# Longer planned distances in a generated schedule, and two stages moved: a hybrid attention and gating block on one core

## Chip, cores and metric

One core of a Trainium2 chip runs the whole program. The metric is the device time of one execution in microseconds (us); lower is better. Engines are named as in the profile: PE is TensorE, DVE VectorE, ACT ScalarE, POOL GpSimd, SP the engine whose queue issues nearly all transfers.

## What is computed

x is 1024 x 1024, float32, one layer, 8 heads of 64 and 8 gating groups of 64. Cut to what matters:

```python
h = rmsnorm(x, norm_g)
q, k, v, z_a, u_b, v_b, z_b, g_a, g_b = split(h @ w_in)      # 1024 -> 5632
# attention: w[t, s] = sigmoid(z[t, s]) * prod over s < r < t of sigmoid(-z[t, r]), s < t
y_a = stick_breaking_attention(q, k, v) * silu(z_a)          # 1024 x 512
y_b = spatial_gating(gelu(u_b), gelu(v_b), ...) * silu(z_b)  # 1024 x 512
merged = sigmoid(g_a) * (y_a @ w_up_a) + sigmoid(g_b) * (y_b @ w_up_b)
out = rmsnorm(x + merged @ w_out, final_norm_g)
```

## The kernel before

**Matrix products.** Every large product is made of three float32r products of high and low parts (hi x hi, lo x hi, hi x lo), 128 x 128 weights against 512 columns. The high part is a copy on ScalarE, the low part a subtraction on VectorE or GpSimd (`hi_lo`).

**Stages.** First x is normalised, transposed and split (`make_h`), and v is projected (`v_unit`, PSUM tiles X, Y, Z, o). Then come 20 projection groups (`project`), each two tiles of 128 output columns made by a seven-product scheme of 12 matmuls each on tiles T; the raw weights are four loads (tile a), their parts tiles b. What leaves a group goes through `use`: kq groups (keys and queries of two heads) are split and stored, u and zb groups make the gated halves of the spatial branch, vb groups normalise and mix (with `mix_weights` and `make_shift`), za groups make the attention branch's SiLU, g groups make sigmoid gates. Results go to DRAM tiles (d) and are read back where needed: zb reads u, vb reads the product uz, a head reads its kq tiles.

**Heads.** Eight heads h0 to h7 run in turn (`head`, `attn_step`, `attn_row`). A head loads the tiles kh, q, kl and v (tag k, `load_head`). For each row block of 128, z = q x kh + q x kl (PSUM z, two buffers), ScalarE makes two sigmoids (tiles ak and r), VectorE a running product along the row (lines 192 and 199), VectorE or GpSimd the weights; TensorE transposes them by blocks of 128 columns (PSUM tr), ScalarE and VectorE split them (tiles e), and TensorE sums them with v in PSUM o. A head's result goes into tile os; for an odd head it is multiplied by the gate and, but for the last pair, stored.

**End.** The up projections of the spatial branch (`up_b`), those of the attention branch for the first and the second half of the sequence (`up_a`), then the output projection and the last norm.

**Who sets the order.** Nothing is issued as it is written. `Plan.add` records each operation as a task with an engine, a cost and its dependencies. `Plan.issue` (line 235) then plays a table of events: each engine takes, of the tasks that are ready and whose buffers are to be had, the one of lowest priority number, and the order in which tasks were taken is the order in which they are issued, engine by engine, and for transfers in SP's queue. On the chip, semaphores make every dependency hold; the table's times count only through the order.

- Costs are formulas per kind of operation; a transfer costs its bytes at 360 GB/s and 0.02 us (lines 219 to 232).
- A task's users become ready at its end, later by `LAT` (line 24) if they are on another engine; behind a transfer they become ready `tail` after its end (lines 225 and 232).
- A buffer comes free `tail` (0 but for transfers) and `LAT` after its last user's end (line 319). The tags have few buffers: k 6, f1 4, f2 6, a 7, b 8, r 5, ak 4, e 4, z 2, tr 2, and one each of X, Y, Z, o. Buffers of a tag are handed out in the order in which the program first names them.
- A task's priority number is its place in the program. For engines other than TensorE an offset is added: -9000 for a projection's own work, and for the work on its results -6000 if the group is marked `+` (`ahead`), else 0. For TensorE the place in the program counts alone: of two groups that are both ready, the one named earlier goes first, and a later group fills in where the earlier one waits.
- The stages between the v projection and the end are named in this list (lines 831 and 832):

```python
    ORDER = ("+kq0 u0 zb0 vb0 +za0 +u1 zb1 +vb1 h0 h1 kq1 h2 g2 +g0 +kq2 +g1 "
             "+kq3 +za1 h3 h4 h5 g6 g3 h6 g4 g5 h7 +g7")
```

h0 and h1 read kq0, h2 and h3 kq1, h4 and h5 kq2, h6 and h7 kq3; h5 and h7 read the results of za1.

Of the kernel before, what the change touches and what calls it, by code (L numbers as in the profile page):

```python
# [20 lines left out]
EPS = 1e-6  # L21
GELU_C = 0.044715
GELU_S = 1.5957691216057308
LAT = 0.25
SCAN = 2.0


# [53 lines left out]
def raw_words(v):  # L81

    return v.ap().bitcast(F32) if v.buf.dt == F32R else v.ap()
# [7 lines left out]
class Plan:  # L91
# [127 lines left out]
    def load(self, out, dram, queue=None):  # L219
        q = queue or self.nc.sync  # L220
        rows = out.box[0][1] - out.box[0][0]
        view = isinstance(dram, View)
        self.add("DMA", out.n * rows * 4 / 360e3 + 0.02,
                 lambda: q.dma_start(out=raw_words(out), in_=dram.ap() if view else dram), [out], [dram] if view else [],  # L224
                 tail=2.0)

    def store(self, dram, in_, queue=None):
        q = queue or self.nc.sync
        view = isinstance(dram, View)
        self.add("DMA", in_.n * P * 4 / 360e3 + 0.02,  # L230
                 lambda: q.dma_start(out=dram.ap() if view else dram, in_=raw_words(in_)), [dram] if view else [], [in_],
                 tail=2.0)


    def issue(self):
# [26 lines left out]
        while done < len(self.tasks):  # L262
# [38 lines left out]
            while events and events[0][0] <= now + 1e-9:  # L301
# [5 lines left out]
                elif kind == 0:  # L307
                    for u in t.users:
                        lag = t.tail if t.eng == "DMA" else 0.0 if u.eng == t.eng else LAT
                        u.ready = max(u.ready, now + lag)  # L310
# [4 lines left out]
                    for b in t.bufs:  # L315
                        b.left -= 1
                        if b.left == 0 and b.tag in free:
                            seq += 1
                            heapq.heappush(events, (now + t.tail + LAT, seq, 2, b.tag))
        self.length = max(t.end for t in self.tasks)  # L320
# [13 lines left out]
def hybrid_block(  # L334
# [489 lines left out]
    def head(p, h):  # L824
        parts = load_head(p, h)
        for ch in range(2):
            if h == 0:
                sums_of[p, ch] = buf("os")
            attn_step(*parts, p, h, ch, sums_of[p, ch])

    ORDER = ("+kq0 u0 zb0 vb0 +za0 +u1 zb1 +vb1 h0 h1 kq1 h2 g2 +g0 +kq2 +g1 "
             "+kq3 +za1 h3 h4 h5 g6 g3 h6 g4 g5 h7 +g7")
    groups_of = {"kq": make_kq, "u": make_u, "zb": make_zb, "vb": make_vb, "za": make_za, "g": make_gates}
    for word in ORDER.split():
        name = word.strip("+0123456789")
# [200 lines left out]
```

## Time and profile before

| what | us |
|---|---|
| median of 3 runs | 774.28 (771.2 to 777.28) |
| the profiled execution | 775.14 |
| its span, first to last instruction | 773.4 |
| TensorE busy | 739.1 |
| VectorE busy | 559.9 |
| ScalarE busy | 433.8 |
| GpSimd busy | 300.7 |

The profile is of one execution; the 1.7 us between its time and its span lie outside the program's instructions. A busy TensorE is a modelled figure: a 128 x 512 matmul is shown with some 390 ns, and back to back one starts every 0.227 us (12 in 2.72 us). Holes are therefore read from the idle time that a timeline shows in brackets, with what ended it, and from the number of matmuls in a window. A granted clock of 1.00 is the engine's upper level (2.4 GHz), 0.50 its lower one (1.2 GHz).

### The profile page before, as it was taken

The numbers are of one execution on the slowest core, as the hardware profiler recorded it, in microseconds if no ns is written. First come the engines' busy times: TensorE is split into PE (matmuls) and PEld (weight loads), VectorE is DVE, ScalarE is ACT, GpSimd is POOL, SyncE is SP. The second block draws the span as 40 slices with busy tenths as digits, with TensorE's granted clock in tenths as the row PEclk, the third lists the DMA queues.
The fourth block names the chain that finished last, engine by engine and source line by source line (L and its number), as shares of the span: only waits on it lengthen the run. The fifth ranks groups of instructions, "written<-read, shape, count | busy, mean of one in ns | idle before, by whom it ended". The sixth has DMA issues, their size and how long they took to land.

```text
span 773.4 us, 10783 instructions
## 1 busy us (share of the span) xinstructions
PE 739.1 (96%) x3524; PEld 609.9 (79%) x3524; DVE 559.9 (72%) x788; ACT 433.8 (56%) x920; POOL 300.7 (39%) x298
## 2 busy tenths in 40 slices
PE   4998999999999999998999999999899999999996
PEld 3776888778887888787888788788688788888885
DVE  5679454797658887976869997879779898961132
ACT  6655474655656466575666576758557544431122
POOL 1400636586677761642556353260321030003110
PEclk9999999999999999999999999999899999999999
DMA  8503593423354463546247354534986636871022
GB/s 325 192 28 122 176 247 123 149 96 123 106 181 131 160 199 102 161 147 164 93 153 205 109 134 126 149 125 144 259 264 222 212 132 211 261 252 74 28 82 109
DMA packets 69177, 121.31 MB, mean 157 GB/s; under 512 B 7296, under 2 KB 17024, under 8 KB 69120
## 3 DMA queue, kind: packets, MB, share of 16 engines
q1 hardware_dynamic: 67968, 118.52, 48.6%
q10 hardware_dynamic: 1152, 2.10, 0.7%
q8 instruction: 28, 0.46, 0.2%
q14 instruction: 29, 0.24, 0.1%
HBM read 81.27 MB, written 39.32 MB: 156 GB/s over the span
## 4 chain that ended last, share of the span: by engine, by line
PE 80%; DMA 7%; issue 4%; DVE 4%; POOL 3%; ACT 1%; SPq 1%; POOLq 0%; DVEq 0%; ACTq 0%
PE Y L131 20%; PE X L131 20%; PE Z L131 17%; PE z L131 9%; PE o L131 9%; PE tr L135 5%; DMA k<-d 4%; DMA k<-in_x_dram 1%; DVE T L168 1%; POOL a L168 1%; SPq L224 1%; POOL f L168 1%; DMA a<-d 1%; DMA a<-in_w_pairs_dram 1%; DVE b L168 1%
## 5 line engine op out<-in xcount | busy, mean ns | idle before, releaser
L131 PE MATMUL Y<-T,b 128*128 128x512 f32 x672 | 180.6, 399 | 2.8 <-ACT b L159 1.6
L131 PE MATMUL X<-T,b 128*128 128x512 f32 x660 | 177.3, 400 | 0.0
L159 ACT CAST b<-a 128x512 fp32r<-128x512 f32 (+1 forms) x152 | 93.3, 615 | 111.0 <-PE X L131 34.9
L131 PE MATMUL Z<-T,b 128*128 128x512 f32 x540 | 147.6, 398 | 0.0
L131 PEld LDWEIGHTS Y<-T,b 128*128 128x128 f32 x672 | 123.1, 190 | 26.2 <-ACT b L159 2.1
L131 PEld LDWEIGHTS X<-T,b 128*128 128x128 f32 x660 | 121.6, 190 | 22.8
L168 DVE TENSOR_TENSOR b<-a,b 128x512 fp32r<-128x512 f32 (+1 forms) x112 | 94.8, 847 | 50.3 <-ACT b L159 46.4
L131 PEld LDWEIGHTS Z<-T,b 128*128 128x128 f32 x540 | 98.2, 188 | 17.9
L168 POOL TENSOR_TENSOR b<-a,b 128x512 fp32r<-128x512 f32 x40 | 58.7, 1469 | 95.6 <-ACT b L159 89.7
L168 POOL TENSOR_TENSOR f<-f,f 128x512 f32<-128x512 f32 (+1 forms) x38 | 58.3, 1538 | 49.4 <-ACT f L148 23.7
L168 POOL TENSOR_TENSOR a<-a,a 128x512 f32<-128x512 f32 x40 | 59.1, 1478 | 30.3 <-DVE b L168 13.5
L168 POOL TENSOR_TENSOR r<-r,ak 128x512 f32<-128x512 f32 x32 | 44.5, 1396 | 64.7 <-DVE ak L192 48.8
L131 PE MATMUL z<-k,k 128*128 128x512 f32 (+2 forms) x216 | 59.9, 358 | 9.4 <-DMA k<-d 8.6
L159 ACT CAST e<-tr 128x512 fp32r<-128x512 f32 (+1 forms) x96 | 45.8, 480 | 36.3 <-PE tr L135 34.1
L168 DVE TENSOR_TENSOR e<-tr,e 128x512 fp32r<-128x512 f32 (+1 forms) x96 | 52.5, 548 | 16.0 <-ACT e L159 15.6
L199 DVE TENSOR_TENSOR_SCAN ak<-ak,c 128x128 f32<-128x128 f32 (+1 forms) x64 | 63.6, 1001 | 0.2 <-ACT ak L148 0.2
L135 PE MATMUL tr<-c,r 128*128 128x128 f32 x320 | 60.9, 275 | 1.5 <-POOL r L168 1.5
L131 PE MATMUL o<-e,k 128*128 128x512 f32 (+1 forms) x192 | 58.4, 348 | 0.0
L148 ACT ACTIVATE ak<-z 128x128 f32<-128x128 f32 (+2 forms) x96 | 47.2, 493 | 16.8 <-PE z L131 11.6
L131 PEld LDWEIGHTS z<-k,k 128*128 128x128 f32 x216 | 40.1, 192 | 18.8 <-issue 5.5
L148 ACT ACTIVATE r<-z 128x128 f32<-128x128 f32 (+2 forms) x96 | 46.8, 493 | 12.2 <-PE tr L135 11.7
L135 PEld LDWEIGHTS tr<-c,r 128*128 128x128 f32 x320 | 41.7, 141 | 15.0 <-POOL r L168 3.0
(217 smaller groups left out, 1158.1 us busy)
## 6 DMA issues: line engine op xcount, KB each, us to landing
d<-f SPq DMA_DIRECT2D x112, 256.0 KB, 2.7
a<-in_w_pairs_dram SPq DMA_DIRECT2D x80, 256.0 KB, 2.7
f<-d SPq DMA_DIRECT2D x72, 256.0 KB, 3.3
k<-d SPq DMA_DIRECT2D x48, 256.0 KB, 4.3
k<-in_x_dram SPq DMA_DIRECT2D x8, 512.0 KB, 6.8
d<-b SPq DMA_DIRECT2D x16, 256.0 KB, 2.3
k<-d SPq DMA_DIRECT2D x8, 512.0 KB, 6.3
a<-in_w_up_dram SPq DMA_DIRECT2D x16, 256.0 KB, 4.6
```

The lines of the kernel that those rows point to most:

```text
L131: lambda: self.nc.tensor.matmul(out.ap(), lhsT=lhsT.ap(), rhs=rhs.ap(), start=start, stop=stop, **kw),
L135: self.add("PE", 0.109, lambda: self.nc.tensor.transpose(out=out.ap(), in_=in_.ap(), identity=ident.ap()), [out], [in_, ident])
L148: return self.nc.scalar.activation(out=out.ap(), in_=in_.ap(), func=func, scale=sc, **kw)
L159: lambda: self.nc.scalar.copy(out=out.ap(), in_=in_.ap()), [out], [in_])
L168: self.add(eng, cost, lambda: e.tensor_tensor(out=out.ap(), in0=in0.ap(), in1=in1.ap(), op=op), [out], [in0, in1])
L199: lambda: self.nc.vector.tensor_tensor_scan(out.ap(), in_.ap(), floor.ap(), init, op0=ALU.mult, op1=ALU.max), [out], [in_, floor])
L224: lambda: q.dma_start(out=raw_words(out), in_=dram.ap() if view else dram), [out], [dram] if view else [],
```

## The change

`LAT` becomes 0.5, the tail of loads and stores 5.0, and the list names u0 before +kq0, and h3 before +kq3 and +za1. No operation and no buffer is added or taken away.

```diff
-LAT = 0.25
+LAT = 0.5
...
     def load(self, out, dram, queue=None):
...
-                 tail=2.0)
+                 tail=5.0)
 
     def store(self, dram, in_, queue=None):
...
-                 tail=2.0)
+                 tail=5.0)
...
-    ORDER = ("+kq0 u0 zb0 vb0 +za0 +u1 zb1 +vb1 h0 h1 kq1 h2 g2 +g0 +kq2 +g1 "
-             "+kq3 +za1 h3 h4 h5 g6 g3 h6 g4 g5 h7 +g7")
+    ORDER = ("u0 +kq0 zb0 vb0 +za0 +u1 zb1 +vb1 h0 h1 kq1 h2 g2 +g0 +kq2 +g1 "
+             "h3 +kq3 +za1 h4 h5 g6 g3 h6 g4 g5 h7 +g7")
```

## Rows read from the trace of the kernel before

**Rows 1.** The page, parts 1 and 2: busy engines, granted clock in 40 slices.

```profile
PE 739.1 (96%) x3524; PEld 609.9 (79%) x3524; DVE 559.9 (72%) x788; ACT 433.8 (56%) x920; POOL 300.7 (39%) x298
...
PEclk9999999999999999999999999999899999999999
```

**Rows 2.** The page, part 4: chain that ended last, by line.

```profile
PE Y L131 20%; PE X L131 20%; PE Z L131 17%; PE z L131 9%; PE o L131 9%; PE tr L135 5%; DMA k<-d 4%; DMA k<-in_x_dram 1%; DVE T L168 1%; POOL a L168 1%; SPq L224 1%; POOL f L168 1%; DMA a<-d 1%; DMA a<-in_w_pairs_dram 1%; DVE b L168 1%
```

**Rows 3.** Windows of 20 us: length, busy us per engine, clock, DMA share, GB/s.

```profile
60.00:80.00 20.00, 17.17 (x75) 13.61 (x74) 18.98 (x23) 11.36 (x18) 2.20 (x2) 1.00 0.35 123
...
340.00:360.00 20.00, 17.52 (x87) 14.23 (x87) 15.74 (x21) 13.65 (x34) 7.78 (x7) 1.00 0.50 140
...
540.00:560.00 20.00, 16.27 (x67) 13.16 (x66) 14.72 (x19) 11.69 (x27) 6.60 (x5) 0.87 0.93 264
...
620.00:640.00 20.00, 20.00 (x106) 16.68 (x105) 18.71 (x27) 9.36 (x23) 6.39 (x5) 1.00 0.42 146
```

**Rows 4.** Tile z on TensorE: waits in all; then TensorE's timeline, two stretches.

```profile
  DMA k<-d: 8.6, 6
...
359.33 0.30 PE L131 MATMUL z<-k,k 128*128 128x128 f32 x1 [2.48 <-DMA k<-d]
...
555.72 0.45 PE L131 MATMUL z<-k,k 128*128 128x128 f32 x1 [3.73 <-DMA k<-d]
```

**Rows 5.** TensorE's waits: line, releaser, us in all, times, longest.

```profile
PE tr L135 <- POOL r L168: 1.5, 2, 1.0
...
PE z L131 <- ACT r L148: 0.8, 1, 0.8
```

**Rows 6.** Timelines of TensorE at 305 us, of SP's queue at 306 and 352 us.

```profile
307.72 0.63 PE L131 MATMUL z<-k,k 128*128 128x512 f32 x2
...
313.49 0.30 PE L131 MATMUL z<-k,k 128*128 128x128 f32 x1 [0.66 <-DMA k<-d]
...
308.67 1.10 SPq L224 DMA_DIRECT2D k<-d  x2
...
353.26 0.38 SPq L231 DMA_DIRECT2D d<-f  x1
```

**Rows 7.** The page, part 6: DMA issues, median us from issue to landing.

```profile
d<-f SPq DMA_DIRECT2D x112, 256.0 KB, 2.7
...
k<-d SPq DMA_DIRECT2D x48, 256.0 KB, 4.3
```

**Rows 8.** Windows at the two long holes, columns as in rows 3.

```profile
360.40:363.80 3.40, 3.40 (x11) 2.68 (x11) 2.67 (x5) 1.90 (x4) 0.00 (x0) 0.50 1.01 245
...
555.00:561.80 6.80, 6.08 (x19) 5.24 (x20) 1.66 (x3) 1.58 (x5) 1.50 (x2) 0.50 0.95 269
```

**Rows 9.** Timeline of all engines at 47 us.

```profile
47.78 0.59 ACT L159 CAST T<-tr 128x512 fp32r<-128x512 f32 x1 [0.64 <-PE tr L135]
...
48.40 1.89 DVE L168 TENSOR_TENSOR T<-tr,T 128x512 f32<-128x512 f32 x3 [0.34 <-ACT T L159]
```

**Rows 10.** The page, part 5: VectorE's subtract for the weights' low parts.

```profile
L168 DVE TENSOR_TENSOR b<-a,b 128x512 fp32r<-128x512 f32 (+1 forms) x112 | 94.8, 847 | 50.3 <-ACT b L159 46.4
```

**Rows 11.** Tile o on TensorE: matmuls of the heads, and TensorE's idle time.

```profile
L131 PE MATMUL o<-e,k x192: 221/389/628, 299.7 to 649.6; 128*128 128x512 f32 x96, 128*128 128x384 f32 x32, 128*128 128x256 f32 x32, 128*128 128x128 f32 x32
...
  ACT e L159: 1.6, 2
```

**Rows 12.** Timelines of SP, ScalarE and TensorE at 138 to 141 us.

```profile
137.83 0.45 SPq L224 DMA_DIRECT2D f<-in_sgu_ln_b_dram  x1
...
140.92 0.30 ACT L159 CAST e<-f 128x128 fp32r<-128x128 f32 x1 [2.62 <-DMA f<-in_sgu_ln_b_dram]
...
141.28 0.39 PE L131 MATMUL o<-b,e 128*128 128x256 f32 x1 [1.16 <-ACT e L159]
```

**Rows 13.** TensorE's timeline where the last head ends.

```profile
649.56 0.39 PE L131 MATMUL o<-e,k 128*128 128x512 f32 x1
...
657.72 0.39 PE L131 MATMUL Y<-T,T 128*128 128x512 f32 x1
```

## The prediction

> **What bounds the kernel now.** I read the page's busy shares and slices first. TensorE is busy 739.1 of 773.4 us; VectorE, the next, 559.9 [rows 1]. The chain that ended last runs mostly over TensorE's lines, and 4% of it is the load of a head's tiles, k<-d, the largest entry that is not TensorE's [rows 2]. Then the 20 us windows, for where TensorE is short of work: 60 to 80 us has 17.17 us busy, 340 to 360 has 17.52 and 540 to 560 has 16.27, while 620 to 640 has 20.00, as all of them have from there to 760 [rows 3]. So what a new order can win lies in single holes before that, and in the granted clock: the slices show 9 everywhere but in one of them [rows 1].
>
> The holes in the heads have one cause. The view of tile z, which every head's first matmuls write, says that TensorE sat idle 8.6 us in 6 places until a k<-d transfer landed; the two longest are 2.48 us before 359.33 and 3.73 us before 555.72 [rows 4]. In the heads' stretch the view of TensorE's waits names little else: 1.5 us on POOL r and 0.8 on ACT r [rows 5].
>
> Why the table misses these: a head takes four tiles k and there are six, so kl and v of the next head can be asked for only when the last z of this one is done. The table then counts 0.25 (LAT) + 2 x 0.73 (two loads of 256 KB at its 360 GB/s) + 2.0 (tail) = 3.7 us to the first matmul on kl, and puts that much projection between. The trace: last z pair starts at 307.72, the loads are issued from 308.67, the matmul on kl starts at 313.49, some 5.2 us after the pair's last matmul (307.72 + 0.23 + 0.3 = 308.25) [rows 6]. A k<-d of 256 KB needs 4.3 us from issue to landing by the median, where the table has 2.73; the stores d<-f of the same size need 2.7 [rows 7].
>
> **The change part by part.** No instruction is added or removed; the three edits only move instructions within each engine's program and within SP's queue.
>
> *Tail 2.0 to 5.0 on loads.* The table's distance to kl grows to 0.5 + 1.46 + 5.0 = 6.96 us, by 3.25. Every one of the six holes shorter than 3.25 us should be filled with projection matmuls, each worth 0.227 us; of the 3.73 us hole 0.5 us is left. 8.6 - 0.5 = **8.1 us saved**. Cover: in each of the seven changes of head some 14 matmuls of projection more must be there to put in. Up to 650 us there are (below).
>
> *The clock.* Directly behind the two long holes the granted clock is at the lower level: 0.50 in 360.40:363.80, where only 11 matmuls start, and 0.50 in 555.00:561.80 with 19 [rows 8]. At half rate, 3.4 us and 6.8 us cost 1.7 + 3.4 = **5.1 us**, which go with the holes. They may stay in part if one hole stays; so between 0 and 5.1, and I take all, since the four shorter holes (8.6 - 2.48 - 3.73 = 2.4 us together) have no such stretch behind them.
>
> *Tail on stores, LAT in the freeing of buffers.* A store's f1, f2 or b buffer counts as taken for 3.25 us longer, so the table hands it out later than the chip does. On the chip the order alone counts, and an order made for later buffers makes nobody wait that did not before; TensorE is given other ready work in that time. I cost it at nothing; if the cover is gone it shows as in the first rival.
>
> *LAT 0.25 to 0.5.* Between engines the chip needs little: VectorE starts at 48.40, 0.03 us after ScalarE ended (47.78 + 0.59) [rows 9]. So 0.25 was long enough where the durations are right; 0.5 gives slack for those that the table has too short: VectorE's subtract b<-a,b takes 847 ns where its formula gives 0.67 us [rows 10]. What it costs in the heads: a block of 128 columns passes TensorE, ScalarE, VectorE and TensorE, three crossings, 0.75 us more in the table; the tiles e (4, two to a block) let two blocks go on together, so 0.375 us a block. The 192 o matmuls [rows 11] are 96 blocks: 36 us of stretch over all heads in the table, if this chain and not VectorE sets a head's pace there. Below: it takes the 1.5 + 0.8 us of short waits away [rows 5]. Above: the order is new everywhere and gets as many short waits again as now. I take the upper end, **2.5 us lost**, for I have no row that says that the new misses will be fewer.
>
> *u0 before +kq0.* In front of zb0 stands then a whole group, 7 products of 2.72 us, instead of nothing, and zb0 reads u back from DRAM. Its reloads take f1 buffers, and vb0's first load into such a buffer, f<-in_sgu_ln_b, is issued only at 137.83; ScalarE waits 2.62 us for it, and TensorE 1.16 us behind ScalarE [rows 12]. All of TensorE's waits for ScalarE at tile o, this one and those of the later vb matmuls, are 1.6 us [rows 11]. kq0 comes 19 us later, its first reader (h0's loads) far behind. Between 0 and 1.6 us saved: I take **0.8**, half, since the buffers are as few as before. In the queues u0's 4 weight loads and 4 stores go ahead of kq0's 4 loads and 8 stores on SP, and the 7 POOL operations of the one ahead of the 7 of the other; nobody else stands between. What 60 to 80 us lacks of 20, 2.8 us [rows 3], stays: whichever group is first finds TensorE waiting until its first weights are split.
>
> *h3 before +kq3 +za1.* TensorE's order is by place in the list, so until now kq3 and za1 went ahead of h3. Now h3 goes ahead of them and 14 products are left over as filler for the heads behind it. Its 7 loads pass in SP's queue the 8 weight loads and 12 stores of the two groups, and need only kq1, stored long before; its 4 POOL products pass work of lower number, which keeps its offset and goes first where it is ready. It moves work, 0 us by itself; it pays some of the time that heads lose through the longer distances.
>
> Sum: -8.1 - 5.1 - 0.8 + 2.5 = -11.5 us. The profiled execution took 775.14 us (span 773.4 and 1.7 around it), so 763.6; it lies 0.9 above the median of 774.28, on which I get 762.8. I say **763 us**.
>
> The Trainium skill has a rule that speaks against the first step: "DMA: Bandwidth & Descriptors", section "Anatomy of one DMA — SWDGE (gpsimd) path", gives one transfer a fixed cost of about 2.0 us and its bytes over 436 GB/s besides, an estimate of 2.6 us for 256 KB. By it the old tail is right, the longer one is needless and nothing is gained. The page's fit is for the GpSimd path and these loads go through SP's queue; the 4.3 us of rows 7 contradict it for k<-d and the 2.7 of the stores agree with it.
>
> **The rivals.** *Heads outlast their filler (slower).* The longer distances keep the heads on for longer while TensorE is fed with projections and up products. What is left when the last head ends is little: its last o is at 649.56, and up to 657.72, where z and the second half's products set in, there are 7.9 us of first-half products [rows 13]. The table adds 7 x 3.25 = 22.75 us at the changes of head and up to 36 us within them, 58.8 in all. If half of it, 29.4 us, reached the chip, TensorE would starve 29.4 - 7.9 = 21.5 us near 650 us, and 775.1 - 11.5 + 21.5 = 785 us. It decides from a stretch of 7.9 + 11.5 = 19.4 us on. For it: VectorE is busy 14.7 to 18.7 of 20 us there [rows 3], so a head can't catch up fast. Against: of the 22.75 us the chip needs the larger part today already (5.2 of 6.96 at each change), and h3 goes earlier.
>
> *Waits that move (no change).* kl lands later still when the order puts other transfers beside it: the DMA share is 1.01 and 0.95 in the stretches where the long holes end [rows 8]. If half of the 8.6 us and the clock's loss stay and the 2.5 us of new waits come, then 775.1 - 4.3 - 0.8 + 2.5 = 772.5 us.
>
> *The old distance was right (no change).* A transfer takes 2.7 us when nothing is beside it, as the stores' row has it [rows 7]; then the holes come of SP's queue, where a store at 353.26 stands ahead of the loads of the hole at 359 [rows 6], and stay: 775 us. The Trainium skill's rule named above would have it so.
>
> **How the numbers follow.** Forecast 0.53; waits that move 0.26; old distance right 0.06; heads outlast the filler 0.15. A measurement of this kernel can tell about 1% from no change, 7.7 us: under 766.5 is faster, over 782.0 slower. The forecast is faster, the two in the middle the same, the last slower: 0.53, 0.32, 0.15. The likeliest one's own range: all gains and no new waits, -8.6 - 5.1 - 1.6 - 2.3 = -17.6, 757; without half of the clock's share and of the holes, 769. For the range of the time I go to 754, for holes before 80 us that may also shut a little, and on the other side to 780, which leaves out most of the last rival.
>
> **What would show it.** Right: the view of tile z names k<-d with under 2 us; no stretch of clock 0.50 after 100 us; windows 340 to 360 and 540 to 560 hold 20.00; the wait of 1.16 us at 141 us is gone; the last head ends later than 649.6 by less than 8 us. The first rival: TensorE idle between 640 and 670 us, waiting for os or T tiles. The second: k<-d's median landing over 5 us and z still waiting. Wrong altogether if z waits less and the time is the same or longer: then the new misses weigh as much as the old.

## The result, and the profile after

| | us |
|---|---|
| before, median | 773.21 |
| changed, median | 761.86 (761.43 to 762.38) |
| ratio | 0.9847, 95% interval 0.9804 to 0.989 |
| span of the profiled execution, before and after | 773.4 and 760.5 |

The changed kernel is 11.4 us, 1.5%, faster; 763 us had been said, within 754 to 780. The median before is of four executions: a fourth of 772.15 us has come to the three behind the 774.28 given above. Both traces are of executions above their medians (775.14 and 762.38 us), so between the traces a little more is won than between the medians. The changed kernel's busy times and its clock, from the page:

```profile
PE 734.5 (97%) x3524; PEld 607.9 (80%) x3524; DVE 563.3 (74%) x788; ACT 432.2 (57%) x920; POOL 304.4 (40%) x298
...
PEclk9999999999999999999999999999999999999999
```

TensorE has the same 3524 matmuls as before and 12.9 us less span [rows 1]; the one slice of clock 8 is gone. Tile z on TensorE, its whole list of waits, beside [rows 4]:

```profile
  DMA k<-d: 0.2, 1
```

The 8.6 us in 6 places are 0.2 in one. The windows that answer to [rows 3]:

```profile
60.00:80.00 20.00, 17.17 (x68) 13.36 (x67) 18.00 (x23) 11.36 (x18) 2.59 (x2) 0.91 0.33 115
...
340.00:360.00 20.00, 20.00 (x102) 16.62 (x100) 15.81 (x26) 14.27 (x35) 2.66 (x6) 1.00 0.41 119
...
540.00:560.00 20.00, 19.91 (x105) 16.50 (x104) 16.87 (x24) 10.89 (x26) 7.45 (x9) 1.00 0.88 280
...
620.00:640.00 20.00, 18.70 (x95) 15.25 (x94) 19.87 (x30) 7.65 (x15) 6.67 (x4) 1.00 0.47 147
```

340 to 360 is full and holds 102 matmuls instead of 87; 540 to 560 has 105 instead of 67 and the clock at 1.00. The holes before 80 us are as before, but the clock behind the one at 70 us is lower (0.91 in this window; the last section comes back to it). What TensorE still waits for, the six longest (line, releaser, us in all, times, longest), beside [rows 5]:

```profile
PE tr L135 <- DVE k L174: 10.3, 2, 7.3
PE Y L131 <- ACT b L159: 2.0, 1, 2.0
PE o L131 <- DVE e L168: 1.5, 2, 1.1
PE X L131 <- ACT r L159: 1.4, 1, 1.4
PE Z L131 <- DVE T L168: 1.3, 1, 1.3
PE tr L135 <- POOL r L168: 1.0, 2, 0.6
```

The first, second and fourth belong to the first 80 us. In the heads' stretch 1.5 + 1.3 + 1.0 = 3.8 us are left. Before it was 1.3 us: 0.8 on ACT r and only 0.5 of the 1.5 us on POOL r [rows 5]. The other 1.0 us of POOL r lies ahead of the heads, which begin at 283.1 us; from the timeline of the kernel before:

```profile
167.86 0.66 PE L135 MATMUL tr<-c,r 128*128 128x128 f32 x4 [1.00 <-POOL r L168]
```

ACT e's 1.6 us [rows 11] lie there too, at 141 and 251 us, and 0.3 us on DVE c at 264: 2.9 us in all, and all of it is gone. So from 100 us on TensorE's waits for anything but k<-d were 4.2 us (2.9 ahead of the heads, 1.3 in them) and are 3.8, all in the heads. Where the last head ends, beside [rows 13]:

```profile
625.77 0.73 PE L131 MATMUL Z<-T,T 128*128 128x512 f32 x2 [1.30 <-DVE T L168]
...
643.29 0.39 PE L131 MATMUL o<-e,k 128*128 128x512 f32 x1
...
645.33 0.62 PE L131 MATMUL z<-T,T 128*128 128x512 f32 x2
```

Between the last o and the first z of the second half's products there are now 2.0 us, where there were 8.6 (from 649.56 [rows 13] to 658.17 in the same timeline); and at 625.77 TensorE stood 1.30 us for a T tile. The cover has shrunk by 6.6 us.

### The profile page after: what moved, and what is told of

It reads as the page before. It is cut to its first block, busy times and chain, and to the rows that moved or that the text cites. A ratio compares the mean times of both kernels' runs of the same rounds, so it can differ in the third digit from the quotient of the medians.

```text
span 760.5 us, 10807 instructions
## 1 busy us (share of the span) xinstructions
PE 734.5 (97%) x3524; PEld 607.9 (80%) x3524; DVE 563.3 (74%) x788; ACT 432.2 (57%) x920; POOL 304.4 (40%) x298
## 4 chain that ended last, share of the span: by engine, by line
PE 85%; DVE 4%; issue 4%; DMA 2%; POOL 2%; ACT 1%; SPq 0%; POOLq 0%; DVEq 0%
PE Y L131 22%; PE X L131 22%; PE Z L131 19%; PE z L131 9%; PE o L131 8%; PE tr L135 5%; DVE T L168 1%; DMA k<-d 1%; DVE ak L192 1%; DMA k<-in_x_dram 1%; POOL a L168 1%; POOL r L168 1%; DMA f<-d 1%; DVE b L168 0%; POOL b L168 0%
## 5 line engine op out<-in xcount | busy, mean ns | idle before, releaser
L131 PE MATMUL Y<-T,b 128*128 128x512 f32 x672 | 182.7, 400 | 2.8 <-ACT b L159 2.0
L131 PE MATMUL Z<-T,b 128*128 128x512 f32 x540 | 145.2, 397 | 0.0
L168 DVE TENSOR_TENSOR b<-a,b 128x512 fp32r<-128x512 f32 (+1 forms) x112 | 100.2, 896 | 47.3 <-ACT b L159 42.1
L168 POOL TENSOR_TENSOR a<-a,a 128x512 f32<-128x512 f32 x40 | 60.9, 1523 | 26.2 <-DVE b L168 21.5
L168 POOL TENSOR_TENSOR r<-r,ak 128x512 f32<-128x512 f32 x32 | 46.6, 1466 | 54.7 <-DVE ak L192 46.0
L168 DVE TENSOR_TENSOR e<-tr,e 128x512 fp32r<-128x512 f32 (+1 forms) x96 | 52.1, 546 | 11.9 <-ACT e L159 11.3
L135 PE MATMUL tr<-c,r 128*128 128x128 f32 x320 | 58.7, 273 | 1.0 <-POOL r L168 1.0
L148 ACT ACTIVATE r<-z 128x128 f32<-128x128 f32 (+2 forms) x96 | 47.1, 494 | 14.3 <-PE tr L135 13.9
L192 DVE TENSOR_TENSOR_SCAN ak<-ak,c 128x512 f32<-128x512 f32 x32 | 50.6, 1594 | 0.0
```

The source lines that it names most:

```text
L131: lambda: self.nc.tensor.matmul(out.ap(), lhsT=lhsT.ap(), rhs=rhs.ap(), start=start, stop=stop, **kw),
L135: self.add("PE", 0.109, lambda: self.nc.tensor.transpose(out=out.ap(), in_=in_.ap(), identity=ident.ap()), [out], [in_, ident])
L148: return self.nc.scalar.activation(out=out.ap(), in_=in_.ap(), func=func, scale=sc, **kw)
L168: self.add(eng, cost, lambda: e.tensor_tensor(out=out.ap(), in0=in0.ap(), in1=in1.ap(), op=op), [out], [in0, in1])
L192: lambda: self.nc.vector.tensor_tensor_scan(out.ap(), in_.ap(), in_.ap(), 1.0 if init is None else init.ap(), op0=ALU.mult, op1=ALU.bypass),
```

## The experiments

Times are medians, in each batch beside the kernel before on the same chip (772.68 us for e1 to e4, 772.47 for e5 to e8, 772.47 for e10 to e13); the changed kernel's 761.86 us is from the run above. In square brackets is the 95% interval of the ratio.

| run | what it is | us | ratio to before |
|---|---|---|---|
| e1_load_tail | before, tail 5.0 on loads | 763.60 | 0.9891 [0.9869, 0.9913] |
| e2_lat | before, LAT 0.5 | 772.42 | 1.0008 [0.9985, 1.0031] |
| e3_order | before, both moves in the list | 776.44 | 1.0052 [1.0033, 1.0072] |
| e4_store_tail | before, tail 5.0 on stores | 771.57 | 0.9990 [0.9974, 1.0006] |
| e5_k_tail | before, tail 5.0 on the heads' loads k<-d alone | 768.21 | 0.9939 [0.9919, 0.9960] |
| e12_other_loads | before, tail 5.0 on all other loads | 768.31 | 0.9943 [0.9924, 0.9963] |
| e10_u0_alone | before, u0 first | 776.60 | 1.0057 [1.0039, 1.0075] |
| e6_undo_k | changed, heads' loads back to 2.0 | 763.71 | 0.9888 [0.9861, 0.9915] |
| e7_no_order | changed, old list | 762.53 | 0.9863 [0.9839, 0.9887] |
| e8_u0_only | changed, h3 back behind +za1 | 761.81 | 0.9856 [0.9835, 0.9877] |
| e11_tail8 | changed, tail 8.0 on loads | 781.81 | 1.0112 [1.0085, 1.0139] |
| e13_lat1 | changed, LAT 1.0 | 785.58 | 1.0164 [1.0137, 1.0191] |

One of e12's five executions took 2619.66 us and is not in its ratio; why is not known.

**One part alone.** My theory (A) was that one distance carries the gain: from a head's loads to its first matmul on kl. The rivals: the distance between engines (B), the list (C), and that any new order moves the holes about by chance (D).

```diff
 e1_load_tail, in load:          -tail=2.0   +tail=5.0
 e2_lat:                         -LAT = 0.25 +LAT = 0.5
 e4_store_tail, in store:        -tail=2.0   +tail=5.0
 e3_order: the changed ORDER
```

> Only the tail of loads goes from 2.0 to 5.0; stores keep 2.0, LAT 0.25, the list is the old one. Theory A (the table's distance from a head's loads to its first matmul on kl was too short, and that is nearly the whole gain): 8.1 us of waits and up to 5.1 us of clock go, new short waits cost up to 2.5; 760 to 766 us, tile z waits under 2 us for k<-d, no stretch of clock 0.50 after 100 us. Rival B (the gain comes of the longer distance between engines): 770 to 775. Rival C (it comes of the list): 770 to 775.

> Only LAT goes from 0.25 to 0.5. Theory A: the distance to kl grows by 0.25 us alone, so 8 us of waits for k<-d stay; 771 to 776 us. Rival B: 760 to 766, with TensorE's short waits for ACT and POOL gone.

> Only the list is changed (u0 before +kq0, h3 before +kq3 +za1). Theory A: 0 to 1.6 us from vb0's wait at tile o; the k<-d waits stay; 771 to 775 us. Rival C: 762 to 768 us. A theory D, that any new order shifts the holes by chance, would have k<-d waits anywhere between 3 and 14 us here, and the time with them.

> Only the tail of stores goes from 2.0 to 5.0. Theory A: nothing in it touches the distance to kl; 771 to 776 us, k<-d waits near 8.6 us. Theory D: anywhere from 766 to 780.

The tail of loads alone gives 9.1 of the 11.4 us. Its view of tile z names no wait at all. LAT alone and the stores' tail alone give nothing that can be told (0.3 and 1.1 us), and the list alone costs 3.8 us. B and C fall. Something of D is true: LAT and the stores leave k<-d waits of 5.3 and 5.1 us, not 8.6, and have more of other waits: from 280 us on 4.1 and 5.2 us, where the kernel before has 1.3.

**Which loads.** Heads' tiles alone, and the complement:

```diff
 e5_k_tail, in load:
-                 tail=2.0)
+                 tail=5.0 if view and out.buf.tag == "k" else 2.0)
 e12_other_loads, in load:
-                 tail=2.0)
+                 tail=2.0 if view and out.buf.tag == "k" else 5.0)
```

> The old kernel with a tail of 5.0 on the heads' loads k<-d alone; all other loads and all stores keep 2.0, LAT 0.25, the old list. Theory A (one distance matters, a head's loads to its first matmul on kl): the whole gain of the run in which all loads had 5.0, so 761 to 766 us, tile z waits under 2 us for k<-d. Rival E (the loads of weights and the reloads f<-d carry a good part): 768 to 772.

> The old kernel with a tail of 5.0 on all loads but the heads' k<-d, which keep 2.0: the other half of the run in which only k<-d had it. That run gave 4.3 us, all loads together 9.1 us. Theory G (the rest comes of loads that ACT, DVE and POOL read: their queues stood still until weights had landed, and the heads' tiles e stood behind them): 766 to 769 us, fewer waits of ACT and POOL for DMA, k<-d waits of tile z still 5 to 9 us. Rival H (the two halves do not add; the rest was a chance of the order): 770 to 775 us.

By the medians each gives about half: 4.3 and 4.2 us, 8.4 together before rounding, as against 9.1 for all loads at once. A in its strict form falls and E holds; of G more below. In e5 the waits for k<-d went as A said, to 1.2 us:

```profile
  DMA k<-d: 1.2, 1
```

but a new hole opened behind them. ScalarE's timeline in e5, and TensorE's at the same time:

```profile
563.12 0.62 ACT L159 CAST T<-a 128x512 fp32r<-128x512 f32 x1 [4.51 <-DMA a<-in_w_up_dram]
563.65 0.58 ACT L159 CAST e<-tr 128x512 fp32r<-128x512 f32 x1
```

```profile
561.16 0.48 PE L131 MATMUL X<-T,b 128*128 128x512 f32 x1
564.28 0.50 PE L131 MATMUL o<-e,k 128*128 128x512 f32 x1 [2.64 <-ACT e L159]
```

ScalarE's next instruction is the copy of an up weight, T<-a, whose load has not landed; it stands there for 4.51 us, and the split of a head's tile e, ready long before, stands behind it. TensorE waits 2.64 us for that e. So a load that TensorE never reads stops it by way of another engine's program. How long ScalarE and GpSimd stood for such transfers in the kernel before, its largest rows from the view of all waits:

```profile
POOL a L168 <- DMA a<-in_w_pairs_dram: 12.7, 2, 10.3
...
ACT T L159 <- DMA a<-in_w_out_dram: 8.6, 7, 2.5
...
POOL f L168 <- DMA f<-d: 7.0, 3, 3.5
...
ACT T L159 <- DMA a<-d: 4.7, 2, 2.9
...
ACT T L159 <- DMA a<-in_w_up_dram: 2.4, 2, 2.2
```

and in the changed kernel, the rows of ScalarE and GpSimd for the same transfers:

```profile
ACT T L159 <- DMA a<-in_w_out_dram: 3.4, 2, 2.1
...
POOL f L168 <- DMA a<-in_w_pairs_dram: 1.8, 1, 1.8
...
ACT T L159 <- DMA a<-in_w_up_dram: 1.1, 2, 0.7
...
POOL f L168 <- DMA f<-d: 0.8, 1, 0.8
...
ACT T L159 <- DMA a<-d: 0.6, 1, 0.6
```

12.7 + 8.6 + 7.0 + 4.7 + 2.4 = 35.4 us have become 3.4 + 1.8 + 1.1 + 0.8 + 0.6 = 7.7; over all rows of ScalarE, VectorE and GpSimd that name a transfer, 57.1 us have become 22.2. How much of it TensorE felt is another matter: before, none of its waits in the heads' stretch names ACT e. In e12 the waits for k<-d stay, shorter than before; the list, and the longest of them:

```profile
  DMA k<-d: 5.0, 5
...
533.52 0.47 PE L131 MATMUL z<-k,k 128*128 128x128 f32 x2 [1.62 <-DMA k<-d]
```

So G is shown only in part. ScalarE and GpSimd wait less for transfers in e12, as it said, and TensorE's waits for anything but k<-d fall from 4.2 to 2.7 us from 100 us on. But most of what e12's trace wins is what A had named: k<-d waits shorter by 3.6 us, and both stretches at 0.50 behind the long holes gone, although the heads' own lead is the old one. Why the longer lead of other loads shortens these holes was not tried. At the longest one before, three loads of up weights go out just ahead of and between the head's k<-d loads in SP's queue (547.7 to 552.4 us); at e12's none does. Since e5 and e12 both lose the two stretches at 0.50, the halves share a part of their gain: between the traces they win 6.5 and 7.8 us of span, e1 11.4. That the medians add up is no proof that they are separate.

**Undoing parts of the change.**

```diff
 e6_undo_k, in load of the changed kernel:
-                 tail=5.0)
+                 tail=2.0 if view and out.buf.tag == "k" else 5.0)
 e7_no_order: the changed kernel with the old ORDER
 e8_u0_only: the changed kernel with
-             "h3 +kq3 +za1 h4 h5 g6 g3 h6 g4 g5 h7 +g7")
+             "+kq3 +za1 h3 h4 h5 g6 g3 h6 g4 g5 h7 +g7")
```

> The changed kernel with the heads' loads k<-d alone back at a tail of 2.0. Theory A: the distance to kl is 0.5 + 1.46 + 2.0 = 3.96 us, so 5 to 9 us of waits for k<-d come back and the clock's loss with them: 768 to 775 us. Rival E: 762 to 766.

> The changed kernel with the old list (distances alone: tails 5.0, LAT 0.5). Theory A: the list is worth little beside the distances: 760 to 766 us. A theory F, by which the two moves only pay with the longer distances (alone they made the kernel 4 us slower): 764 to 770.

> The changed kernel with u0 before +kq0, but h3 left behind +kq3 and +za1. If the h3 move gives filler to the later heads (the prediction's reason for costing it at nothing or better): 762 to 768 us, with a hole of TensorE near the last head's end. If it does nothing: 761 to 763.

Without the heads' tail the changed kernel loses 1.9 us, not the 6 to 13 that A wanted; k<-d waits come back, but in seven short ones:

```profile
  DMA k<-d: 4.1, 7
```

The longest is 1.2 us, and from 100 us to TensorE's last matmul no stretch at 0.50 comes back with them.

The old list costs 0.7 us and h3's old place nothing; the runs of these three kernels lie over one another (761.68 to 762.84, 760.91 to 762.40, 761.43 to 762.38), so the list is worth nothing that can be told here. e7, all distances and no list, has nearly the whole gain.

**Why the list alone costs 4 us.**

```diff
 e10_u0_alone:
-    ORDER = ("+kq0 u0 zb0 vb0 ...
+    ORDER = ("u0 +kq0 zb0 vb0 ...
```

> The old kernel with u0 before +kq0 alone. If the wait of 3.1 us for DVE f at 126 us, which both moves together had with the old distances, comes of u0 going first: 774 to 777 us and the same wait. If it comes of the h3 move: 771 to 773.

It is u0 alone: 4.1 us. The timelines of SP's queue, VectorE and TensorE in e10:

```profile
115.34 5.37 SPq L224 DMA_DIRECT2D k<-d  x4
120.80 0.54 SPq L224 DMA_DIRECT2D a<-in_w_spatial_dram  x1
```

```profile
125.51 0.17 DVE L713 MEMSET a<- 64x128 f32 x1 [6.93 <-DMA a<-in_w_spatial_dram]
125.71 0.69 DVE L168 TENSOR_TENSOR b<-a,b 128x512 fp32r<-128x512 f32 x1
```

```profile
129.51 3.01 PE L131 MATMUL Y<-T,b 128*128 128x512 f32 x12 [1.83 <-DVE f L168]
...
145.99 0.39 PE L131 MATMUL o<-b,e 128*128 128x256 f32 x1 [2.59 <-ACT e L159]
```

The heads' loads k<-d, whose kq0 now comes a group later, stand in SP's queue at 115 to 120 us, ahead of the load of w_spatial. VectorE's next instruction is the memset on that tile; it waits 6.93 us for it, with the weights' split and a result behind it, and TensorE waits 1.83 us for VectorE, later 2.59 for ScalarE. With tail 5.0 on loads the memset is planned later, and the hole is not there: TensorE's timeline of the changed kernel names no wait between 80 and 300 us.

**More of the same.**

```diff
 e11_tail8, in load of the changed kernel:   -tail=5.0   +tail=8.0
 e13_lat1, in the changed kernel:            -LAT = 0.5  +LAT = 1.0
```

> The changed kernel with a tail of 8.0 on loads. If 5.0 covers the landings, more distance only takes filler from the end: 761 to 766 us, and 10 us more than the changed kernel's if the heads outlast their filler as the prediction's first rival had it (7 x 3.0 = 21 us of the table's time more at the changes of head against 8 us of cover).

> The changed kernel with LAT 1.0 in place of 0.5: the stretch of the heads that the prediction put at up to 36 us in the table for 0.25 would be 72 us more. If the heads outlast their filler: 775 to 800 us with TensorE idle near the last head's end. If VectorE and not this chain sets the heads' pace, the order changes little: 760 to 768 us.

Both are slower than the kernel before, by 9.3 and 13.1 us, and than the changed one by 20.0 and 23.7. e11 is above both times that were named for it, e13 in the range named for heads that outlast their filler. The windows from 600 to 680 us (length; busy us of TensorE, weight loads, VectorE, ScalarE, GpSimd; clock; DMA share; GB/s), first the changed kernel, then e11, then e13:

```profile
600.00:620.00 20.00, 20.00 (x104) 16.67 (x104) 18.34 (x29) 14.97 (x39) 2.33 (x5) 1.00 0.60 195
...
640.00:660.00 20.00, 20.00 (x90) 16.57 (x89) 18.74 (x30) 10.56 (x19) 1.79 (x1) 1.00 0.78 236
660.00:680.00 20.00, 20.00 (x89) 16.54 (x89) 16.60 (x29) 8.20 (x16) 2.12 (x4) 1.00 0.96 326
```

```profile
600.00:620.00 20.00, 18.80 (x101) 15.29 (x100) 19.43 (x29) 12.42 (x35) 5.80 (x9) 1.00 0.65 190
620.00:640.00 20.00, 13.59 (x57) 9.21 (x55) 19.09 (x28) 14.00 (x38) 8.67 (x8) 0.85 0.00 0
640.00:660.00 20.00, 19.94 (x93) 16.07 (x92) 16.29 (x27) 9.60 (x17) 0.86 (x2) 0.98 0.51 165
660.00:680.00 20.00, 18.03 (x79) 14.55 (x78) 19.93 (x33) 10.17 (x19) 1.20 (x1) 1.00 0.83 265
```

```profile
600.00:620.00 20.00, 14.12 (x62) 9.98 (x61) 18.00 (x24) 13.13 (x36) 5.43 (x8) 0.83 0.58 167
620.00:640.00 20.00, 15.12 (x76) 10.69 (x75) 17.89 (x29) 14.69 (x41) 3.40 (x9) 0.91 0.02 5
640.00:660.00 20.00, 16.46 (x69) 13.32 (x70) 16.23 (x22) 8.36 (x17) 3.55 (x4) 0.83 0.25 79
660.00:680.00 20.00, 19.76 (x88) 16.03 (x87) 19.74 (x32) 11.98 (x22) 1.80 (x1) 1.00 0.80 263
```

With the changed kernel's own row for 620 to 640 above, TensorE is busy 78.7 of 80 us there; in e11 70.4, in e13 65.5, with the clock down to 0.83 in places. In e11 VectorE is busy 19 of 20 us from 600 to 640 us, DMA does nothing from 620 to 640, and TensorE's waits there name VectorE's e and r for 3.9 us and ScalarE for 3.6: it looks as if the last heads run at the pace of these engines, VectorE's above all, and TensorE has no other work. The prediction's first rival is real; it begins somewhere between the distances of this change and those of e11 and e13, and nothing between was run. Not all of e11's loss is the rival's: at 199.11 us TensorE waits 2.59 us for VectorE's f, and the granted clock is 0.57 in the 4 us from 200. How long the heads last, from tile z and tile o on TensorE in e11 (first and last start):

```profile
L131 PE MATMUL z<-k,k x216: 220/389/628, 310.9 to 726.8; 128*128 128x512 f32 x60, 128*128 128x128 f32 x22, 128*128 128x384 f32 x16, 128*128 128x256 f32 x10
```

```profile
L131 PE MATMUL o<-e,k x192: 220/389/686, 332.2 to 654.0; 128*128 128x512 f32 x96, 128*128 128x384 f32 x32, 128*128 128x256 f32 x32, 128*128 128x128 f32 x32
```

From the first z to the last o it is 654.0 - 310.9 = 343.1 us, in the changed kernel 643.3 - 288.9 = 354.4, before 649.6 - 283.1 = 366.5. So e11's heads are not longer: they begin 22.0 us later than the changed kernel's. That projections and the end's other fillers are used up meanwhile is inferred from the order. In e13 they begin at 298.1 and end at 664.4, 366.3 us: 9.2 later and 11.9 longer. What holds h0 back in e11 wasn't tried.

## Why the prediction was right, and where only by its sum

- **The cause of the long holes: right.** In every run with tail 5.0 or more on the heads' loads, tile z waits 0 to 1.2 us for k<-d (e1, e5, e7, e8, e11, e13 and the changed kernel); in every run with 2.0, 4.1 to 9.0 us (before, e2, e3, e4, e6, e10, e12). 8.1 us were to go and 8.4 went.
- **The clock: right for the traced executions.** Both stretches at 0.50 behind the long holes are gone, 5.1 us. They go too in e12, where k<-d waits of up to 1.6 us stay: it was the long holes that had them. Between medians it must be less: the traced execution of the kernel before has a mean granted clock of 0.989, the 21 beside e1 have 0.992 by the median, and 0.003 of 771 us is some 2 us, an estimate, that most executions did not have to lose.
- **Tail on loads: the sum near, the account too narrow.** The step hung all of the 13.2 us on the heads' tiles. The heads' tail by itself (e5) is worth 4.3 us by the medians. Its 7.4 us of waits and the clock's 5.1 go, but TensorE's waits for anything but k<-d rise from 4.2 to 8.4 us from 100 us on: ACT e has 4.6 instead of 1.6 us, and a wait of 1.5 us for ScalarE's T is new. The step left out the readers of all other loads, which stand at the head of ScalarE's, VectorE's and GpSimd's programs, and that the lead of those loads moves the heads' holes as well: by itself (e12) it is worth 4.2 us and takes the same two stretches at 0.50. With both (e1) the k<-d waits are 0 and the others 4.8 us.
- **The 2.5 us of new waits: right where they were put, too large in the balance.** In the heads' stretch other waits were 1.3 us, not the 1.5 + 0.8 us that the step read from [rows 5], and are 3.8: 2.5 us more. But 2.9 us ahead of the heads are gone, where the step on u0 had 0.8. So other waits came out at 0.4 us saved, where the sum had 1.7 lost.
- **The sum: near, in part by luck.** Between the traces 12.9 us of span went, by the terms 8.4 + 5.1 + 0.4 = 13.9, where 11.5 was forecast. Between the medians 11.4 went, since the traced execution before is 1.9 us above its median and the changed one's 0.5. What the forecast had too much of new waits and what the clock gives less between medians are, by that estimate, of like size; this is how 763 us came so near.
- **Tail on stores, at nothing: right in size** (1.1 us, within the interval), but not since nobody waits who did not before: e4 has 2.8 us on ACT f at 541 us, which the kernel before has not. **LAT: 0.3 us, within the interval.** In e2's trace all of the 2.9 us ahead of the heads are gone and the other waits from 280 us on are 2.7 us more. The stretch of the heads that was put at up to 36 us did not show at 0.5 (they last 354.4 us, before 366.5); at 1.0 they are 11.9 us longer.
- **u0 first, 0.8 us saved: wrong by itself.** It costs 4.1 us in the old table and nothing in the new. The step looked at f1 buffers and zb0's reload, and not at the heads' loads, which wait for kq0 and now fall together with vb0's; for the queue it said that nobody else stands between. The wait of 1.16 us at 141 us is gone, as the step had it, but in e7, with the old list, and in e2, with LAT alone, it is gone too. **h3 first, at nothing: right** (e8), though the reason given for it, filler for the later heads, was not seen.
- **The last head.** It was to end later than 649.6 us and ended at 643.3. Seen from the end of the span it is 6.6 us later (773.4 - 649.6 = 123.8 us before the end, now 760.5 - 643.3 = 117.2). The rival's place was right, its price not: in e11 the heads begin 22.0 us later and are not longer, so the time is not lost at seven changes of head.
- **The other signs.** Windows 340 to 360 and 540 to 560 hold 20.00 and 19.91 us, and from 100 us to TensorE's last matmul no stretch is at 0.50. Of the second rival's two signs one came, k<-d's median landing over 5 us (5.4), but tile z no longer waits.
- **The rule weighed against the trace.** By the fixed cost of the Trainium skill's page "DMA: Bandwidth & Descriptors", section "Anatomy of one DMA — SWDGE (gpsimd) path", a tail of 2.0 was right. e1 decides against it as a planning figure here: 763.60 us with 5.0, 772.68 with 2.0. The stores' 2.7 us [rows 7] are a median over 112 transfers; no run here times a k<-d with nothing beside it.

Open: what the changed kernel has over e1, some 2 us (11.4 and 9.1), is not assigned to LAT, stores or list, none of which can be told alone.

## What to carry to other kernels

Where a table of costs sets an in-order program, the lead given to a transfer should cover the landings under load that the trace shows, and for every load, not only for those that the busiest engine reads: whichever engine has a reader at the head of its program stops all that stands behind it. Once the waits are covered, more lead cost time here (20.0 us in e11), it seems by spending filler; look how much independent work is left where the last dependent chain ends (here 8.6 us before, 2.0 after) before adding any. Moves in such a list are worth judging only in the table that they will run with.

## What the runs showed that was not expected

The heads' transfers land later in the changed kernel than before, and it does not matter. The page's row on them:

```profile
k<-d SPq DMA_DIRECT2D x48, 256.0 KB, 5.4
```

5.4 us by the median instead of 4.3 [rows 7]; e1 has 4.3, e2, with LAT alone, 5.2. The changed kernel's lead of 6.96 us covers it (tile z waits 0.2 us); e2's lead is 3.96 us, and there tile z still waits 5.3.

The clock does not follow a hole of one length every time. Around 70 us the changed kernel and e8 have the same two holes (1.99 and 0.83 us; 1.98 and 0.84). Windows right behind them, the changed kernel's and then e8's:

```profile
72.60:76.00 3.40, 3.40 (x10) 2.58 (x10) 3.33 (x6) 1.07 (x2) 0.00 (x0) 0.53 0.32 80
76.00:80.00 4.00, 4.00 (x19) 3.30 (x18) 2.15 (x3) 2.27 (x5) 2.59 (x2) 1.00 0.19 66
```

```profile
72.00:76.00 4.00, 3.68 (x16) 3.07 (x17) 3.97 (x6) 1.39 (x4) 0.00 (x0) 1.00 0.37 139
```

One falls to the lower level for some 3.4 us, 10 matmuls where the other's 4.0 us hold 16, and the other stays at 1.00. A difference of 1.7 us between two such kernels can be this alone. Nor does the longer hole always cost more: the one of 2.48 us in the kernel before had 0.50 behind it [rows 8], the one of 2.64 us in e5 had not:

```profile
564.28:567.70 3.42, 3.42 (x17) 2.85 (x18) 3.25 (x5) 3.42 (x9) 0.20 (x2) 1.00 0.69 214
```
